# One more block of queries and keys as a unit of tokens with groups of seven products, turned on PE, and the attention heads run later

## The chip, the cores and the metric

The kernel runs on one core of a Trainium2 chip. A core has a matrix engine (PE), a vector engine (DVE), a scalar engine (ACT), a general engine (POOL) and a queue engine that issues most loads (SP). The metric is the device time of one execution in microseconds (us); less is better.

## The reference

One decoder layer for 256 tokens of 2048 features. Both head groups read one projection, and their outputs are concatenated:

```
u = RMSNorm(h)
P = u @ W_in                 # columns [z | x,B,C | dt | q | k | v]
SSD heads:  conv + SiLU on x,B,C; Mamba-2 scan; gate SiLU(z); RMSNorm
attention:  16 heads of 128, causal, three dilated patterns merged
            by their softmax denominators
h = h + RMSNorm(concat(SSD, attn) @ W_out)
h = h + RMSNorm(W_down @ relu(W_up @ RMSNorm(h))^2)
```

All values are 32-bit floats. q, k and v have 2048 columns each, so four blocks of 512 columns, each with four heads.

## The kernel before

**Products.** Each 32-bit factor is split into a high part (ACT, line 147) and a low part (DVE, line 148), and a product of two factors is three matmuls: high by high, low by high, high by low. Weights come in tiles of 256 rows by 512 columns: SP loads a tile into a "raw" buffer (line 161), ACT and DVE make "hi" and "lo" of it, of which there are five buffers each. A step over 256 rows is called a k here; w_in has eight of them. There are three forms of a product:

- *features* (`gemm_features`, lines 473 and 476): the weights stand still and the tokens stream, so the result has features on the partitions. High weights take 512 columns, which hold both parts of 256 tokens, and low weights take 256. Eight matmuls of each for a k and a column block.
- *tokens*, plain (`row_tile`, lines 328 to 330): the tokens stand still and 512 weight columns stream; 12 matmuls for a k and a column block. The text calls these 12 a tile.
- *tokens*, by seven (`seven`, lines 411 to 413): for a k and two column blocks, seven products of halves replace eight, so 21 matmuls instead of 24. DVE adds up halves of the two raw tiles first (line 252: into "e" and "r"), and sums of the activations are made once for each k (lines 368 to 371).

A *unit* makes two column blocks in the tokens form over all k, some plain and some by seven; its sums lie in four "acc" results and four "more" results, and at its end they are combined on DVE (lines 421 to 424). Results lie in PSUM, which has eight banks: six of the pool "acc" (`bank()`) and two of the pool "ps" (`psmall()`).

**Queries, keys, values.** q and k are wanted with features on the partitions. Block 0 is made as features. Block 1 is made as a unit (queries and keys are its two column blocks; k = 1, 3, 5, 6 by seven), and its 16 pieces of 128 x 128 are then turned with transposes on PE (line 921). Blocks 2 and 3 are made as features (`queries`, added up at line 497 and scaled at line 896). The values are made in two units of two blocks (V0 and V2; sums at lines 966 and 967).

**Attention.** `attention` is a generator for a lane, a pair of heads, in three steps. Step 1: scores of both heads on PE (854, 855) into two "ps" banks; DVE takes masked maxima (862), ACT the exponentials (864), DVE reciprocals and scaling (866, 868). Step 2: transposes on PE (876) into two "ps" banks, copied by ACT (880). Step 3: products with the values on PE (885, 886) into one "ps" bank, split into "ah" and "al" by ACT (147) and DVE (148). `heads` puts the two lanes of a block of four heads into the queue `waiting`. `pump(n)` runs the next step of n lanes in turn; the products call it after each k or tile, by the tuple `pumps`. Every step of PE, DVE and ACT has its place in its engine's queue before the run.

**Order before.** Features of block 0; the unit QK1 of block 1; V0, in which QK1's results are turned; Q2 and K2 as features, with heads 0 and heads 1 beside them; V2; Q3 and K3 as features, with heads 2; then the first five k of w_out in two column blocks as ten plain tiles (EARLY = 5), with heads 3; then a unit with the rest of w_out's k for these two blocks. That unit begins once the pool "ap" of the heads is closed; ACT then issues the loads of "wpost" and of x (lines 1264 to 1269). Its order is k = 5, 6, 7, 8, 9, 11, 10, 13, 12, of which 6, 8, 9, 10 and 12 are by seven.

**Places beside the pools.** While no heads run, the space of attention's outputs ("ah0" and "al0", `not_yet`) holds four further raw tiles, so there are eight; the rows of a unit and the places of DVE's additions are tiles "tk" and "cT" of the middle pool.

Of the kernel before, what the change touches and what calls it, by code (L numbers as in the profile page):

```python
# [10 lines left out]
F32 = mybir.dt.float32  # L11
# [5 lines left out]
P = 128  # L17
S = 256
# [21 lines left out]
KB = 2  # L40
# [37 lines left out]
def hymba_layer(ctx: ExitStack, tc: tile.TileContext, x, norm_mix_pre, w_in, conv_w, conv_b, dt_bias, a_log,  # L78
# [239 lines left out]
    def drain():  # L318
        while waiting:
            pump()  # L320
# [104 lines left out]

    for n in (0, 2):
        plan("v", w_v, n, range(7), V_SEVENS)
    plan("out", w_out, 0, (5, 6, 7, 8, 9, 11, 10, 13, 12), (6, 8, 9, 10, 12))
    plan("out", w_out, 2, (0, 6, 1, 9, 2, 12, 3, 4, 5, 8, 7, 10), (6, 9, 12, 4, 8, 10))
    for hf in range(2):  # L430
        for n in range(0 if hf else 2, 8, 2):
# [473 lines left out]
            sums_of_acts(k)  # L905
            yield

    def place_of_sums():

        room["sum"] = mp.tile([P, 4, S], F32, name="cT", bufs=5).rearrange("p (k f) s -> p k (f s)", k=KB)  # L910

    def eight_banks():
        more = [psmall(), bank(), psmall(), bank()]
        return [bank() for _ in range(2 * NT)], more

    def turned_heads(t, dst, r, p, later):
        for _ in range(later):
# [6 lines left out]
    def keys_by_tokens(hb, order, last, acc, more):  # L924

        room["own"] = deque(mp.tile([P, NT, NB], F32, name="tk", bufs=3)[:, t] for t in range(NT))
        if hb == 1:
            place_of_sums()
            rstq.append(mp.tile([P, NT], F32, name="rstq"))
            nc.vector.tensor_scalar(rstq[0], rstd, DH ** -0.5, None, op0=ALU.mult)  # L930
        rows, both = [], []

        def ready():
            if not more:
                more.extend(f() for f in (psmall, bank, psmall, bank))
# [12 lines left out]
        unit(w_in, (COL_Q + hb * NB, COL_K + hb * NB), order_of(order, QK_SEVENS), last, acc, more,  # L948
             lambda x: combine_new([[v[:, t] for t in range(NT)] for v in rows], x), 0, (end(0), end(1)),
             ready=ready)  # L950
        return both
# [2 lines left out]

    def two_values(vb, acc, more):

        room["own"] = deque(mp.tile([P, NT, NB], F32, name="tk", bufs=3)[:, t] for t in range(NT))
        if vb:
            place_of_sums()
        values = [mp.tile([P, NT, NB], F32, name="tk", bufs=3) for _ in range(2)]  # L960

        def end(b):
# [22 lines left out]
    ap_ = ExitStack()  # L985
    ap = ap_.enter_context(tc.tile_pool(name="ap", bufs=2, side="right", reuse_waits="tile"))
# [7 lines left out]
    qk.append(keys_by_tokens(1, (0, 2, 1, 3, 4, 5, 6), (7,), *eight))  # L994
    vs = two_values(0, *eight[::-1])
    room["raw"], room["turn"] = [], 0
    att[0] = [bigr.tile([P, NK // 2, S], F32R, name=name) for name in ("ah0", "al0")]
# [12 lines left out]

# [467 lines left out]
```

## Time and profile before

| | |
|---|---|
| median of 3 runs | 1458.33 us (1457.78 to 1458.51) |
| the profiled execution | 1458.42 us, its span 1456.6 us |
| mean granted clock of PE | 0.999 |
| PE busy | 1448.5 us, 99% of the span |
| DVE busy | 1268.3 us, 87% |
| ACT busy | 897.8 us, 62% |
| HBM read and written | 248 GB/s over the span |

Times in rows are counted from the span's start. A row of the timeline has start, length, engine, line, operation, the written and read tiles, shape, count, and in brackets the idle time of the engine before it and who ended it. The length of a matmul is longer than its distance to the next, since matmuls overlap; distances between starts give what PE needs.

### The profile page before, as it was taken

What the parts mean: (1) busy time and instruction counts of PE and PEld (TensorE: products, weight loads), DVE (VectorE), ACT (ScalarE), POOL (GpSimd) and SP (SyncE); (2) the same over time, 40 slices, a digit from 0 to 9 for tenths busy, and PEclk for the clock granted to TensorE, in tenths of its full rate; (3) what the DMA queues carried; (4) which work ended last, traced back from release to release, by engine and by line L of the source; (5) the groups of instructions that cost most, each with busy time, mean ns of one, the idle gap of its engine ahead of it and who ended that gap; (6) DMA issues with size and microseconds to landing.
All of it is one profiled execution on the core that took longest, in us unless ns stands there. A gap on an engine that the chain in (4) does not pass through costs nothing.

```text
span 1456.6 us, 20308 instructions
## 1 busy us (share of the span) xinstructions
PE 1448.5 (99%) x7117; PEld 1222.2 (84%) x7117; DVE 1268.3 (87%) x1886; ACT 897.8 (62%) x1227; POOL 146.2 (10%) x214
## 2 busy tenths in 40 slices
PE   9999999999999999999999999999999999999998
PEld 8888888888888888888888888888888888888886
DVE  6798897798987686689878999999889999999997
ACT  7465665465666556556557577666454776766663
POOL 0003100211110000001100111011111111101000
PEclk9999999999999999999999999999999999999999
DMA  8766666567875486688876798678888888798854
GB/s 270 209 205 179 184 179 197 178 175 231 237 224 174 130 235 209 191 255 270 260 226 216 205 313 242 193 227 253 241 248 279 251 245 245 210 293 263 250 176 159
DMA packets 168758, 325.10 MB, mean 223 GB/s; under 512 B 15328, under 2 KB 18256, under 8 KB 168656
## 3 DMA queue, kind: packets, MB, share of 16 engines
q1 hardware_dynamic: 144496, 272.37, 58.3%
q0 software_dynamic: 16288, 37.76, 13.2%
q10 hardware_dynamic: 7872, 13.68, 2.7%
q8 instruction: 56, 0.92, 0.2%
q14 instruction: 46, 0.38, 0.1%
HBM read 319.53 MB, written 41.98 MB: 248 GB/s over the span
## 4 chain that ended last, share of the span: by engine, by line
PE 99%; DVE 0%; ACT 0%; issue 0%; ACTq 0%
PE acc L473 15%; PE acc L328 12%; PE acc L330 12%; PE acc L329 12%; PE acc L476 8%; PE acc L413 6%; PE acc L411 6%; PE acc L412 6%; PE ps L330 3%; PE ps L329 3%; PE ps L328 3%; PE ps L413 2%; PE ps L411 2%; PE ps L412 2%; PE ps L807 1%; PE acc L1385 1%
## 5 line engine op out<-in xcount | busy, mean ns | idle before, releaser
L147 ACT ACTIVATE hi<-raw 128x1024 fp32r<-128x1024 f32 (+1 forms) x392 | 409.8, 1051 | 268.6 <-PE acc L473 92.2
L148 DVE TENSOR_TENSOR lo<-raw,hi 128x1024 fp32r<-128x1024 f32 (+1 forms) x392 | 476.9, 1221 | 92.7 <-ACT hi L147 88.7
L473 PE MATMUL acc<-ua,hi 128*128 128x512 f32 x600 | 163.5, 401 | 0.0
L473 PEld LDWEIGHTS acc<-ua,hi 128*128 128x128 f32 x600 | 105.7, 189 | 16.7
L147 ACT ACTIVATE hi<-e 128x1024 fp32r<-128x1024 f32 x64 | 68.0, 1063 | 71.4 <-DVE e L252 66.3
L328 PE MATMUL acc<-hi,ua 128*128 128x512 f32 x248 | 98.4, 397 | 0.0
L330 PE MATMUL acc<-hi,ua 128*128 128x512 f32 x248 | 96.8, 390 | 0.0
L476 PEld LDWEIGHTS acc<-ua,lo 128*128 128x128 f32 x600 | 88.2, 189 | 10.3
L329 PE MATMUL acc<-lo,ua 128*128 128x512 f32 x248 | 96.7, 390 | 0.0
L476 PE MATMUL acc<-ua,lo 128*128 128x256 f32 x600 | 90.8, 281 | 0.0
L328 PE MATMUL acc<-hi,sh 128*128 128x512 f32 x224 | 88.4, 395 | 0.0
L330 PE MATMUL acc<-hi,sl 128*128 128x512 f32 x224 | 87.3, 390 | 0.0
L329 PE MATMUL acc<-lo,sh 128*128 128x512 f32 x224 | 87.2, 389 | 0.0
L148 DVE TENSOR_TENSOR lo<-e,hi 128x1024 fp32r<-128x1024 f32 x64 | 77.9, 1218 | 0.0
L473 PE MATMUL acc<-uc,hi 128*128 128x512 f32 x240 | 68.5, 397 | 0.0
L411 PE MATMUL acc<-hi,ah 128*128 128x512 f32 x174 | 67.8, 389 | 0.0
L412 PE MATMUL acc<-lo,ah 128*128 128x512 f32 x174 | 67.7, 389 | 0.0
L413 PE MATMUL acc<-hi,al 128*128 128x512 f32 x174 | 67.7, 389 | 0.0
L148 DVE TENSOR_TENSOR lo<-ha,hi 128x1024 fp32r<-128x1024 f32 x43 | 52.4, 1220 | 6.0 <-ACT hi L147 5.7
L147 ACT ACTIVATE hi<-ha 128x1024 fp32r<-128x1024 f32 x43 | 45.3, 1057 | 18.3 <-PE acc L330 9.8
L330 PEld LDWEIGHTS acc<-hi,ua 128*128 128x128 f32 x248 | 46.6, 188 | 10.0
L328 PEld LDWEIGHTS acc<-hi,ua 128*128 128x128 f32 x248 | 46.6, 188 | 9.4 <-ACT ua L149 0.3
(543 smaller groups left out, 3510.9 us busy)
## 6 DMA issues: line engine op xcount, KB each, us to landing
raw<-in_w_in_dram SPq DMA_DIRECT2D x167, 512.0 KB, 3.9
raw<-in_w_down_dram SPq DMA_DIRECT2D x72, 512.0 KB, 5.2
raw<-in_w_up_dram SPq DMA_DIRECT2D x65, 512.0 KB, 4.6
raw<-in_w_out_dram SPq DMA_DIRECT2D x38, 512.0 KB, 5.0
pair<-in_w_up_dram POOLq DMA_DIRECT2D x56, 256.0 KB, 5.3
pair<-in_w_down_dram POOLq DMA_DIRECT2D x50, 256.0 KB, 6.3
raw<-pair SPq DMA_DIRECT2D x46, 256.0 KB, 4.6
ha<-in_w_up_dram SPq DMA_DIRECT2D x20, 512.0 KB, 5.7
```

What stands on the lines that cost most here:

```text
L147: return (nc.scalar.activation(hi, src, AF.Copy), nc.vector.tensor_tensor(lo, src, hi.bitcast(F32), op=ALU.subtract))
L148: nc.vector.tensor_tensor(lo, src, hi.bitcast(F32), op=ALU.subtract))
L328: nc.tensor.matmul(dst, a_h[:, r, ts], hi[:, j], start=begin and j == 0, stop=False)
L329: nc.tensor.matmul(dst, a_h[:, r, ts], lo[:, j], start=False, stop=False)
L330: product[t] = nc.tensor.matmul(dst, a_l[:, r, ts], hi[:, j], start=False, stop=end and j == KB - 1)
L411: nc.tensor.matmul(dst, a_h, hi[:, j], start=own and first, stop=False)
L412: nc.tensor.matmul(dst, a_h, lo[:, j], start=False, stop=False)
L413: nc.tensor.matmul(dst, a_l, hi[:, j], start=False, stop=own and last)
L473: nc.tensor.matmul(acc[f], hi[:, j, f * P:(f + 1) * P], u(k0 + j), start=k0 + j == 0, stop=False, skip_group_check=True)
L476: nc.tensor.matmul(acc[f][:, 0], lo[:, j, f * P:(f + 1) * P], u(k0 + j)[:, 0], start=False, stop=k0 + j == NK - 1, skip_group_check=True)
L807: nc.tensor.matmul(p[:, c, r], bc[:, r, c * P:(c + 1) * P], xdt[:, c, r], start=True, stop=True)
L1385: nc.tensor.transpose(p[:, f * P:(f + 1) * P], r[:, f * P:(f + 1) * P], ident)
```

## The change

- Block 2's queries and keys become a unit like block 1's (`keys_by_tokens(2, ...)`, after V0), four k of seven by seven in the order 0, 2, 1, 3, 4, 5, 6 and then 7. Its 16 pieces are turned on PE (line 923) beside the first k of Q3.
- For these units the places of DVE's additions and one further raw tile lie in a new pool `tp` of three tiles; the pool `ap` of the heads is opened only after them. The rows of the units lie in "al0", so three further raw tiles remain instead of four: seven raw buffers in all. The banks of "acc" and "more" are dealt out the other way round.
- Heads 0 run beside Q3 and heads 1 beside K3 (features), with new `pumps`. Heads 2 and 3 both run beside the ten tiles of w_out: `heads` takes several blocks, and a lane goes on with block 3 after block 2.
- w_out's first unit has its k in the order 5, 7, 6, 9, 8, 11, 10, 13, 12, with the same five by seven.

The core of the diff:

```diff
-    plan("out", w_out, 0, (5, 6, 7, 8, 9, 11, 10, 13, 12), (6, 8, 9, 10, 12))
+    plan("out", w_out, 0, (5, 7, 6, 9, 8, 11, 10, 13, 12), (6, 8, 9, 10, 12))
...
     def eight_banks():
-        more = [psmall(), bank(), psmall(), bank()]
-        return [bank() for _ in range(2 * NT)], more
+        acc = [f() for f in (bank, psmall, bank, psmall)]
+        return acc, [bank() for _ in range(2 * NT)]
...
-            rows[:] = [mp.tile([P, NT, NB], F32, name="tk", bufs=3) for _ in range(2)]
-            both[:] = [mp.tile([P, 4, S], F32, name="cT", bufs=5) for _ in range(2)]
+            rows[:] = [not_yet[1][:, t:t + NT] for t in (0, NT)]
+            both.append(mp.tile([P, 4, S], F32, name="cT", bufs=5))
+            both.append(mp.tile([P, 4, S], F32, name="cT", bufs=5) if hb == 1 else
+                        mp.tile([P, NT, NB], F32, name="tk", bufs=3).rearrange("p t (f s) -> p (t f) s", s=S))
...
-    def heads(hb, qT, kT, v):
+    def heads(*blocks):
+        def lane(j):
+            for i, (hb, qT, kT, v) in enumerate(blocks):
+                if i:
+                    yield
+                yield from attention(ap, 4 * hb + j, qT[:, j:j + 2], kT[:, j:j + 2],
+                                     v[:, :, j * DH:(j + 2) * DH].rearrange("p t (j d) -> p t j d", j=2))
         for j in (0, 2):
-            waiting.append(attention(ap, 4 * hb + j, qT[:, j:j + 2], kT[:, j:j + 2],
-                                     v[:, :, j * DH:(j + 2) * DH].rearrange("p t (j d) -> p t j d", j=2)))
+            waiting.append(lane(j))
...
-    room["raw"], room["turn"], room["acts"] = [t[:, k:k + KB] for t in not_yet for k in (0, KB)], 0, act_u
+    room["raw"], room["turn"], room["acts"] = [not_yet[0][:, k:k + KB] for k in (0, KB)] + [more_raw], 0, act_u
...
     vs = two_values(0, *eight[::-1])
+    qk.append(keys_by_tokens(2, (0, 2, 1, 3, 4, 5, 6), QK_SEVENS, (7,), *eight))
...
-    heads(0, *qk[0], vs[0])
-    q2 = queries(COL_Q + 2 * NB, rbq, (1,0,1,1,0,1,1,1))
+    for _ in range(NT):
+        bank()
+    heads((0, *qk[0], vs[0]))
+    q3 = queries(COL_Q + 3 * NB, rbq, (1, 2, 1, 0, 1, 1, 2, 1))
     drain()
-    heads(1, *qk[1], vs[1])
-    qk.append((q2, queries(COL_K + 2 * NB, rbc, (1, 1, 0))))
-    drain()
+    heads((1, *qk[1], vs[1]))
+    qk.append((q3, queries(COL_K + 3 * NB, rbc, (1, 1, 0, 1, 1, 1, 1, 0))))
...
-    heads(2, *qk[2], vs[2])
-    qk.append(keys_too(3, (1, 0)))
-    heads(3, *qk[3], vs[3])
+    for _ in range(NT):
+        bank()
+    heads(*((hb, *qk[hb], vs[hb]) for hb in (2, 3)))
...
-            row_tiles(w_out, b * NB, [k], acc[b::2], part, k == 0, False, pumps=1,
+            row_tiles(w_out, b * NB, [k], acc[b::2], part, k == 0, False, pumps=(1, 1, 1, 1, 1, 2, 1, 2, 1, 1)[2 * k + b],
                       fetch=fetch_next)
```

Three places in the queues show what moves. The first is PE after V2. Before, the features of Q3 followed, and between the scores of heads 2's lane 0 (the first four rows; "ps" are the two banks) and those of lane 2 (the last four) stood two k of features:

```order
L854 MATMUL ps<-cT 128x128
L855 MATMUL ps<-cT 128x256
L854 MATMUL ps<-cT 128x128
L855 MATMUL ps<-cT 128x256
L473 MATMUL acc<-ua,hi 128x512 x8
L476 MATMUL acc<-ua,lo 128x256 x8
L473 MATMUL acc<-ua,hi 128x512 x8
L476 MATMUL acc<-ua,lo 128x256 x8
L854 MATMUL ps<-cT 128x128
L855 MATMUL ps<-cT 128x256
L854 MATMUL ps<-cT 128x128
L855 MATMUL ps<-cT 128x256
```

Now the tiles of w_out follow ("sh" and "sl" are the two parts of the SSD output), and between these scores stands one tile. Its last three matmuls and lane 2's scores:

```order
L328 MATMUL acc<-hi,sh 128x512
L329 MATMUL acc<-lo,sh 128x512
L330 MATMUL acc<-hi,sl 128x512
L854 MATMUL ps<-tk,cT 128x128
L855 MATMUL ps<-tk,cT 128x256
L854 MATMUL ps<-tk,cT 128x128
L855 MATMUL ps<-tk,cT 128x256
```

Lane 2's scores, which use the two "ps" banks again, have moved one k closer to those of lane 0.

The second place is DVE from the end of V2 to the maxima of the first scores. Before:

```order
L966 TENSOR_TENSOR tk<-acc,tk 128x512
L148 TENSOR_TENSOR lo<-raw,hi 128x1024
L966 TENSOR_TENSOR tk<-acc,tk 128x512 x2
L148 TENSOR_TENSOR lo<-raw,hi 128x1024 x4
L862 ISA sm,mx<-ps,cst 128x128
L862 ISA mx 128x1
L862 ISA sm,mx<-ps,cst 128x256
L862 ISA mx 128x1
L862 ISA sm,mx<-ps,cst 128x128
```

Now:

```order
L963 TENSOR_TENSOR tk<-acc,tk 128x512
L148 TENSOR_TENSOR lo<-raw,hi 128x1024
L963 TENSOR_TENSOR tk<-ps,tk 128x512 x2
L148 TENSOR_TENSOR lo<-raw,hi 128x1024 x4
L862 ISA sm,mx<-ps,cst 128x128
L862 ISA mx 128x1
L862 ISA sm,mx<-ps,cst 128x256
L862 ISA mx 128x1
L862 ISA sm,mx<-ps,cst 128x128
```

The order of additions (966 is now 963), low parts and maxima stayed the same, while the low parts are now those of w_out.

The third place is where heads 0 run. On PE, their second steps (transposes, line 876, of lane 0 and then of lane 2). Before, in Q2:

```order
L876 MATMUL ps<-ident,sm 128x128 x6
L473 MATMUL acc<-ua,hi 128x512 x8
L476 MATMUL acc<-ua,lo 128x256 x8
L473 MATMUL acc<-ub,hi 128x512 x8
L476 MATMUL acc<-ub,lo 128x256 x8
L876 MATMUL ps<-ident,sm 128x128 x6
L473 MATMUL acc<-uc,hi 128x512 x8
L476 MATMUL acc<-uc,lo 128x256 x8
```

Now, in Q3:

```order
L876 MATMUL ps<-ident,sm 128x128 x6
L473 MATMUL acc<-uc,hi 128x512 x2
L476 MATMUL acc<-uc,lo 128x256 x2
L473 MATMUL acc<-uc,hi 128x512
L876 MATMUL ps<-ident,sm 128x128 x4
L473 MATMUL acc<-uc,hi 128x512
L876 MATMUL ps<-ident,sm 128x128 x2
L476 MATMUL acc<-uc,lo 128x256 x2
```

Two k of features stood between the two lanes' transposes, and now five matmuls do, and one more stands inside those of lane 2.

On DVE, the low parts ahead of the first maxima of heads 0. Before:

```order
L148 TENSOR_TENSOR lo<-raw,hi 128x1024
L966 TENSOR_TENSOR tk<-acc,tk 128x512 x2
L148 TENSOR_TENSOR lo<-raw,hi 128x1024 x4
L862 ISA sm,mx<-ps,cst 128x128
L862 ISA mx 128x1
```

Now:

```order
L148 TENSOR_TENSOR lo<-raw,hi 128x1024
L943 TENSOR_TENSOR al_3683<-ps,al_3683 128x512
L148 TENSOR_TENSOR lo<-raw,hi 128x1024 x8
L862 ISA sm,mx<-ps,cst 128x128
L862 ISA mx 128x1
```

Four low parts in a row stood there behind the last additions for the values (966), and now eight stand behind the last addition for the new unit's keys (943).

More of the change, by code (lines that the diff above doesn't have):

```diff
@@ L906, in sums_ahead, with own_places @@
             yield
-    def place_of_sums():
-        room["sum"] = mp.tile([P, 4, S], F32, name="cT", bufs=5).rearrange("p (k f) s -> p k (f s)", k=KB)
+    def own_places(tiles):
+        own, total = tiles
+        room["own"] = deque(own[:, t] for t in range(NT))
+        room["sum"] = total
     def eight_banks():
-        more = [psmall(), bank(), psmall(), bank()]
-        return [bank() for _ in range(2 * NT)], more
+        acc = [f() for f in (bank, psmall, bank, psmall)]
+        return acc, [bank() for _ in range(2 * NT)]
     def turned_heads(t, dst, r, p, later):
@@ L922, in turned_heads, with keys_by_tokens @@
         nc.scalar.activation(dst[:, :, t * P:(t + 1) * P], p.rearrange("p (f s) -> p f s", f=4), AF.Copy)
-    def keys_by_tokens(hb, order, last, acc, more):
-        room["own"] = deque(mp.tile([P, NT, NB], F32, name="tk", bufs=3)[:, t] for t in range(NT))
+    def keys_by_tokens(hb, order, sevens, last, acc, more):
         if hb == 1:
-            place_of_sums()
             rstq.append(mp.tile([P, NT], F32, name="rstq"))
@@ L946, in end @@
             return at_end
-        unit(w_in, (COL_Q + hb * NB, COL_K + hb * NB), order_of(order, QK_SEVENS), last, acc, more,
+        unit(w_in, (COL_Q + hb * NB, COL_K + hb * NB), order_of(order, sevens), last, acc, more,
              lambda x: combine_new([[v[:, t] for t in range(NT)] for v in rows], x), 0, (end(0), end(1)),
@@ L984, in hymba_layer @@
     not_yet = [bigr.tile([P, 2 * KB, NB], F32, name=name) for name in ("ah0", "al0")]
-    ap_ = ExitStack()
-    ap = ap_.enter_context(tc.tile_pool(name="ap", bufs=2, side="right", reuse_waits="tile"))
+    tp_ = ExitStack()
+    tp = tp_.enter_context(tc.tile_pool(name="tp", bufs=1, side="right", reuse_waits="tile"))
+    more_raw, *of_sums = [tp.tile([P, KB, NB], F32, name=f"tp{i}") for i in range(3)]
+    own_places(of_sums)
     room["sums"] = [v[:, k:k + KB] for k in range(0, NK // 2, KB) for v in att[1]]
-    room["raw"], room["turn"], room["acts"] = [t[:, k:k + KB] for t in not_yet for k in (0, KB)], 0, act_u
+    room["raw"], room["turn"], room["acts"] = [not_yet[0][:, k:k + KB] for k in (0, KB)] + [more_raw], 0, act_u
     waiting.append(sums_ahead())
@@ L993, in hymba_layer @@
     eight = eight_banks()
-    qk.append(keys_by_tokens(1, (0, 2, 1, 3, 4, 5, 6), (7,), *eight))
+    qk.append(keys_by_tokens(1, (0, 2, 1, 3, 4, 5, 6), QK_SEVENS, (7,), *eight))
     vs = two_values(0, *eight[::-1])
+    qk.append(keys_by_tokens(2, (0, 2, 1, 3, 4, 5, 6), QK_SEVENS, (7,), *eight))
     room["raw"], room["turn"] = [], 0
+    tp_.close()
     att[0] = [bigr.tile([P, NK // 2, S], F32R, name=name) for name in ("ah0", "al0")]
-    heads(0, *qk[0], vs[0])
-    q2 = queries(COL_Q + 2 * NB, rbq, (1,0,1,1,0,1,1,1))
+    ap_ = ExitStack()
+    ap = ap_.enter_context(tc.tile_pool(name="ap", bufs=2, side="right", reuse_waits="tile"))
+    for _ in range(NT):
+        bank()
+    heads((0, *qk[0], vs[0]))
+    q3 = queries(COL_Q + 3 * NB, rbq, (1, 2, 1, 0, 1, 1, 2, 1))
     drain()
-    heads(1, *qk[1], vs[1])
-    qk.append((q2, queries(COL_K + 2 * NB, rbc, (1, 1, 0))))
-    drain()
+    heads((1, *qk[1], vs[1]))
+    qk.append((q3, queries(COL_K + 3 * NB, rbc, (1, 1, 0, 1, 1, 1, 1, 0))))
+    own_places([mp.tile([P, 4, S], F32, name="cT", bufs=5).rearrange("p (k f) s -> p k (f s)", k=KB) for _ in range(2)])
     vs += two_values(2, *eight_banks())
-    heads(2, *qk[2], vs[2])
-    qk.append(keys_too(3, (1, 0)))
-    heads(3, *qk[3], vs[3])
+    for _ in range(NT):
+        bank()
+    heads(*((hb, *qk[hb], vs[hb]) for hb in (2, 3)))
     del room["own"], room["sum"]
```

5 lines of the change are left out of this document (removed).

## The prediction

> **What bounds the kernel now.** I read the page first, for the bound; then the chain of work that ended last; then a table of stretches, one for each stage around the change; then the timeline of single engines at the places where the new order differs. The page says:
>
> ```profile
> span 1456.6 us, 20308 instructions
> PE 1448.5 (99%) x7117; PEld 1222.2 (84%) x7117; DVE 1268.3 (87%) x1886; ACT 897.8 (62%) x1227; POOL 146.2 (10%) x214
> PE 99%; DVE 0%; ACT 0%; issue 0%; ACTq 0%
> ```
>
> PE is busy for 1448.5 of 1456.6 us and 99% of the chain runs over it. So two things alone count: how long PE's own work is, and whether a new wait opens in it. DVE, at 87%, is the engine that could open one. The stages (columns: length, then busy time of PE, PEld, DVE, ACT, POOL with counts, granted clock, DMA share, GB/s):
>
> ```profile
> 360.20:401.25 41.05, 41.05 (x184) 34.02 (x183) 40.27 (x54) 24.90 (x30) 7.03 (x10) 1.00 0.91 249
> 401.25:443.92 42.67, 42.67 (x198) 35.45 (x196) 38.61 (x45) 29.03 (x34) 4.07 (x6) 1.00 0.70 197
> 443.92:501.75 57.83, 57.83 (x346) 51.46 (x344) 36.88 (x90) 34.17 (x70) 1.35 (x2) 1.00 0.56 164
> 501.75:542.61 40.86, 40.86 (x183) 33.82 (x182) 35.65 (x42) 23.92 (x26) 4.09 (x6) 1.00 0.77 217
> 542.61:593.87 51.26, 51.26 (x302) 45.35 (x301) 34.56 (x61) 28.96 (x51) 0.00 (x0) 1.00 0.64 197
> ```
>
> In order: the unit of the second block's queries and keys (QK1); the first unit of values (V0), which also turns QK1's results on PE; the third block's queries and keys as features (Q2, K2) with two blocks of heads; the second unit of values (V2); the fourth block's queries and keys (Q3, K3) with one block of heads. PE is busy in all of each, at full clock.
>
> **The work that PE loses and gains.** The third and fifth rows are the same two features, with two blocks of heads and with one. Their difference, 57.83 - 51.26 = 6.57 us, is one block of heads on PE, and 51.26 - 6.57 = 44.69 us is a pair of features alone. That is removed for block 2. In its place comes a unit like QK1; V2 is a unit with nothing beside it, 40.86 us. Its 16 transposes are the difference between V0 and V2: 42.67 - 40.86 = 1.81 us. The heads keep their length wherever they run. Sum: -44.69 + 40.86 + 1.81 = -2.02 us. All of it is on the path, since PE has no slack.
>
> **The new unit's cover.** A group of seven costs DVE more than PE, so the unit lasts 40.86 us only if DVE starts it with a lead. Rows of DVE around the end of V0, which is where the new unit begins (443.92 is its first matmul's time; the first row is the low part of the unit's second tile, the other that of tiles three to six):
>
> ```profile
> 442.37 1.21 DVE L148 TENSOR_TENSOR lo<-raw,hi 128x1024 fp32r<-128x1024 f32 x1
> 444.73 4.79 DVE L148 TENSOR_TENSOR lo<-raw,hi 128x1024 fp32r<-128x1024 f32 x4
> ...
> 443.24 0.39 PE L328 MATMUL acc<-hi,uc 128*128 128x512 f32 x1
> 443.92 0.61 PE L473 MATMUL acc<-ua,hi 128*128 128x512 f32 x2
> ```
>
> Three matmuls of 512 columns take 0.68 us (443.24 to 443.92), 0.227 each, 2.72 for the 12 of a plain tile, 4.76 for the 21 of a seven. The second tile's low part is done at 443.58 and would be used at about 446.9: a lead of 3.3 us. Each plain tile adds 2.72 - 1.14 = 1.58 (four low parts in 4.79 us, 1.14 a step after the first); four come before the first two sevens and two before the last two. A seven in this projection takes DVE three low parts of 1.14, one of 0.6 and four or five additions of 0.6, up to 6.4, so two cost 3.3. The lead stays above 3 us: no stall. QK1, with DVE 40.27 of 41.05 busy, shows that this runs without a wait. The seven raw buffers instead of eight I cost at nothing for the same lead; without it each late load would cost its lateness.
>
> **Heads 2 and 3 beside the first products of w_out.** Here a wait is added. After V2 the order on DVE is as before: the last sums of the values, four low parts, then the first masked maximum (L862). Rows of before, where heads 2 start at the same point:
>
> ```profile
> 545.31 3.48 DVE L148 TENSOR_TENSOR lo<-raw,hi 128x1024 fp32r<-128x1024 f32 x3
> 549.60 1.23 DVE L148 TENSOR_TENSOR lo<-raw,hi 128x1024 fp32r<-128x1024 f32 x1 [0.81 <-ACT hi L147]
> 550.74 0.28 DVE L862 CUSTOM_DVE_ANT_0 sm<-ps,cst 128x128 f32<-128x128 f32 x1
> 550.95 0.42 DVE L862 CUSTOM_DVE_ANT_0 sm<-ps,cst 128x256 f32<-128x256 f32 x1
> 551.51 0.42 DVE L862 CUSTOM_DVE_ANT_0 sm<-ps,cst 128x256 f32<-128x256 f32 x1
> ...
> 545.38 0.38 PE L854 MATMUL ps<-cT 128*128 128x128 f32 x2
> 552.28 0.39 PE L854 MATMUL ps<-cT 128*128 128x128 f32 x2
> ```
>
> The scores of lane 0 stand in the two "ps" banks from 545.38; DVE has read the first bank at about 551.3. The scores of lane 2 need these banks and came at 552.28, behind two tiles, so nothing waited. Now they come behind one. The lengths, from the heads of block 3 in the same stage:
>
> ```profile
> 593.86 0.40 PE L328 MATMUL acc<-hi,sh 128*128 128x512 f32 x1
> 596.61 0.38 PE L854 MATMUL ps<-cT 128*128 128x128 f32 x2
> 597.73 0.58 PE L328 MATMUL acc<-hi,sh 128*128 128x512 f32 x1
> 598.15 0.40 PE L329 MATMUL acc<-lo,sh 128*128 128x512 f32 x1
> ```
>
> A step of scores takes 597.73 - 596.61 = 1.12, and its next matmul 0.42 instead of 0.23. Set on the old clock: 542.61 + 2.72 + 1.31 + 2.72 = 549.36 is when PE reaches lane 2's scores, and 551.3 when the bank is free: a wait of 2.0 us. Behind the waiting matmul stands all of PE's queue; DVE is ahead and only gains by it. Ends: 0, if the low parts come 2 us sooner because w_out's load is not the one that ACT waited for; 4, if the fourth of them slips by a landing. I take 2.0 since order and engines are the same, and 0.2 for later steps, where transposes follow the other lane's maximum closely: 2.2.
>
> **Heads 0 beside Q3.** Before, the two transposing steps were two k apart (457.71 and 463.96); now the second stands five matmuls behind the first, and eight low parts in a row stand ahead of the first maximum.
>
> ```profile
> 457.71 0.82 PE L876 MATMUL ps<-ident,sm 128*128 128x128 f32 x6
> 463.96 0.82 PE L876 MATMUL ps<-ident,sm 128*128 128x128 f32 x6
> 448.28 1.28 ACT L864 ACT_TABLE_LOAD   x1
> 449.76 0.40 ACT L864 ACTIVATE sm<-sm,mx 128x128 f32<-128x128 f32 x1 [0.20 <-DVE mx L862]
> 451.11 0.49 ACT L864 ACTIVATE sm<-sm,mx 128x256 f32<-128x256 f32 x1
> 459.35 0.84 ACT L880 ACTIVATE pT<-ps 128x384 f32<-128x384 f32 x2
> ```
>
> Let lane 0's scores start at 0. The last of the eight low parts waits for one of the five buffers, which frees there: ACT's high part 1.06, DVE's low part done at 2.5, maxima to 3.7. PE: scores 1.3, tile of 2.8, scores, tile, first transposes at 8.2. ACT has by then eight exponentials (0.58 and 0.68 with their read-outs) and two high parts; the last exponential ends at about 11, the first copy of transposed weights at 11.4. Lane 0's second head waits for lane 2's last maximum (9.2 against 8.5): 0.7. Lane 2's transposes need the bank that this copy frees: 11.5 against 10.5 to 10.9. Together 1.0 to 1.9; I take 1.5. Ends: 0, if ACT's high part goes ahead by half a tile, and 2.5, if one more lands between the exponentials. K3 with heads 1 keeps two tiles between these steps: nothing.
>
> **The output unit.** Its order has four plain tiles, then three sevens in a row (before: two in a row). From before (a seven's first addition, the next row after its last part, a plain tile's low part; then that tile on PE):
>
> ```profile
> 644.75 0.69 DVE L252 TENSOR_TENSOR e<-raw 128x512 f32<-128x512 f32 x1
> 650.68 0.68 DVE L368 TENSOR_TENSOR r<-ah,al 128x512 f32<-128x512 f32 x1
> 651.29 1.22 DVE L148 TENSOR_TENSOR lo<-uc,hi 128x1024 fp32r<-128x1024 f32 x1
> 652.42 0.42 DVE L369 TENSOR_TENSOR r<-r 128x256 f32<-128x256 f32 x1
> ...
> 653.30 0.39 PE L329 MATMUL acc<-lo,ah 128*128 128x512 f32 x1
> ```
>
> A seven takes DVE 5.9 (644.75 to 650.68) against 4.76 on PE; after two of them the low part was done at 652.51 and used at 653.30, 0.8 us later. Now DVE begins the sums when the last head's step ends, at E, since the place of the first sum waits for PE. From there to the low part behind the third seven stand ten operations of 1024 columns, nineteen of 512, three of 256 and six of 128 (1.14, 0.6, 0.34, 0.2): 25.0 us, so done at about E + 25.2. PE has four tiles, three sevens and one matmul: 10.9 + 14.3 + 0.3 = E + 25.5. The lead is 0.3; I take 0.2 us of stall. Ends: 0, and 3 where DVE's start or a high part comes late.
>
> With the end of the heads ACT issues the loads of x, before ahead of the last four tiles, now at the unit's start:
>
> ```profile
> 618.06 0.45 ACTq L1268 DMA_DIRECT2D ha<-in_x_dram  x1
> ha<-in_x_dram ACTq DMA_DIRECT2D x1, 1536.0 KB, 12.0
> ```
>
> They take the DMA engines for 12 us. The weights of the three sevens are asked for as buffers come free, four tiles (10.9 us) and more ahead of their use, so I cost this at nothing; if a seven's load slips past that cover, it adds to DVE's lateness below.
>
> **Sum.** -2.02 + 2.2 + 1.5 + 0.2 = +1.9 us on the profiled execution's 1458.42 us (span 1456.6 and 1.8 around it): 1460.3. The median of the runs shown is 0.09 below it, so 1460.2. I call under 0.2% (2.9 us) no change, which is about what a measurement of this kernel tells apart: 1455.4 to 1461.2.
>
> **Rivals.** *The waits do not come.* Then the gain stands alone: 1458.33 - 2.02 = 1456.3, with partial waits up to 1458.3. For it: no stage here shows PE waiting. Against: both waits follow from orders that are fixed before the run, with durations from this trace.
>
> *The output unit's third seven is late (slower).* The lead there is 0.3 us, so DVE's lateness beyond that is PE's, one for one. Seen: in this stage DVE has no gap at all between additions. The result is slower from 1.3 us of stall on (1460.2 - 0.2 + 1.3 = 1461.3); if DVE begins 2.8 us late, one tile on PE, 2.5 us are lost: 1462.5.
>
> *The clock drops during a wait.* PE's records at the end (windows: columns as above):
>
> ```profile
> 1450.40 1.13 PE L1330 MATMUL ps<-mw,dg 128*128 128x512 f32 x2 [1.70 <-ACT dg L1329]
> ...
> 1447.70:1450.40 2.70, 1.01 (x3) 0.18 (x1) 2.00 (x5) 1.42 (x4) 0.00 (x0) 1.00 0.54 190
> 1453.50:1454.00 0.50, 0.00 (x0) 0.00 (x0) 0.00 (x0) 0.00 (x0) 0.00 (x0) 0.80 1.06 373
> 1454.00:1455.00 1.00, 0.00 (x0) 0.00 (x0) 0.00 (x0) 0.00 (x0) 0.00 (x0) 0.50 0.43 162
> ```
>
> An idle stretch of 1.7 us kept 1.00; after the last matmul (to 1451.53) the clock went to 0.50 about 2.3 us later. A wait of 2.0 lies between. If the clock then stays at half for as long as the wait again and a little more, say 3 us, 1.5 us are lost: 1461.7. [...]
>
> [...]
>
> **Chances.** The forecast 0.56; waits absent or mostly so 0.17; output unit late 0.2; clock 0.07. The forecast's own range is 1458.5 to 1462, of which a quarter is above 1461.2. Of the second case a third is put under 1455.4, for which PE's work must be another 0.9 us shorter than counted. Of the third, 0.16 lies above 1461.2. So faster 0.05, same 0.58, slower 0.14 + 0.16 + 0.07 = 0.37. The range takes the second case from 1456.0 and the third up to 1464.0, which leaves about 0.15 outside.
>
> **What would show it.** Right: the unit of block 2 takes 40.9 us with no PE wait; an idle row of about 2 us on PE before lane 2's scores, released by L862, in the stage of w_out; one of 0.7 to 1.9 in sum on the transposes in Q3, released by L862 or the copy L880; DVE without gaps in the output unit. Wrong: a unit longer than 41.5 (DVE or loads late), no wait at the scores (low parts earlier), more than 1.1 us of PE waiting at the third seven, or a granted clock under 1.00 anywhere between 360 and 700 us.

## The result and the profile after

The changed kernel takes 1462.28 us in the median of seven runs (1459.8 to 1464.39), the kernel before beside it 1458.33 us (1457.68 to 1458.53). The ratio is 1.0028, its interval 1.0018 to 1.0038: slower by 0.28%. That is above the 0.2% taken as measurable, so the change made the kernel slower. (The ratios in this text are worked out from the single executions and need not be those of the medians.) The profiled execution takes 1462.42 us, 4.00 more than the one before, and the waiting is in one place. The page after:

```profile
span 1460.6 us, 20239 instructions
PE 1449.4 (99%) x7057; PEld 1219.1 (83%) x7057; DVE 1283.0 (88%) x1906; ACT 905.9 (62%) x1236; POOL 146.5 (10%) x214
PE 96%; DVE 3%; ACT 1%; issue 0%; ACTq 0%
```

PE has 60 instructions less than before and yet is busy for 0.9 us more, which says that some of its work ran slower. In the chain of work that ended last, DVE and ACT now hold 4%. The stages (columns as in the prediction): QK1 and V0 together; the new unit; Q3 and K3 with two blocks of heads; V2; the ten tiles of w_out with two blocks of heads; the start of the output unit.

```profile
360.37:444.38 84.01, 83.94 (x378) 69.04 (x377) 80.52 (x103) 53.62 (x63) 10.16 (x14) 1.00 0.86 243
444.38:485.18 40.80, 40.80 (x181) 33.80 (x180) 39.99 (x49) 26.06 (x30) 0.00 (x0) 1.00 0.57 165
485.18:545.09 59.91, 59.91 (x362) 53.16 (x361) 36.80 (x88) 35.80 (x73) 1.36 (x2) 1.00 0.56 161
545.09:585.90 40.81, 40.81 (x183) 33.78 (x182) 36.78 (x45) 22.79 (x25) 4.10 (x6) 1.00 0.76 212
585.90:631.64 45.74, 42.74 (x209) 35.44 (x208) 28.85 (x75) 28.64 (x60) 2.71 (x4) 0.96 0.66 206
631.64:660.00 28.36, 28.36 (x128) 23.48 (x127) 28.04 (x44) 17.30 (x22) 2.73 (x4) 1.00 0.84 252
```

The fifth row shows PE idle for 3.00 of 45.74 us (the first for 0.07, which is taken up with QK1 below, the others for none), and only there is the granted clock below 1.00. PE's timeline in that stage:

```profile
592.24 0.39 PE L329 MATMUL acc<-lo,sh 128*128 128x512 f32 x1
592.47 0.39 PE L330 MATMUL acc<-hi,sl 128*128 128x512 f32 x1
595.85 0.49 PE L854 MATMUL ps<-tk,cT 128*128 128x128 f32 x2 [3.00 <-DVE mx L862]
596.18 0.60 PE L855 MATMUL ps<-tk,cT 128*128 128x256 f32 x2
...
598.03 0.63 PE L329 MATMUL acc<-lo,sh 128*128 128x512 f32 x1
598.46 0.63 PE L330 MATMUL acc<-hi,sl 128*128 128x512 f32 x1
```

The scores of heads 2's lane 2 wait 3.00 us for lane 0's maximum (L862). By starts, 3.385 us (592.47 to 595.85) instead of 0.227 costs 3.16 us. Behind it a matmul step takes 0.43 (598.03 to 598.46) instead of 0.23. The windows around that stretch:

```profile
596.75:597.00 0.25, 0.25 (x4) 0.25 (x3) 0.25 (x2) 0.25 (x1) 0.00 (x0) 0.83 1.18 344
597.00:597.25 0.25, 0.25 (x3) 0.17 (x2) 0.25 (x2) 0.25 (x1) 0.00 (x0) 0.50 0.99 320
...
600.25:600.50 0.25, 0.25 (x3) 0.20 (x2) 0.25 (x2) 0.25 (x1) 0.00 (x0) 0.84 0.92 147
```

A window of 0.25 us with a mean of 0.83 was at full clock for two thirds of it, so the clock fell to half at 596.92; the same reading of the last row puts its return at 600.33. That is 3.41 us at half, 1.7 us of PE's time. Against the prediction's terms, stage by stage, in us:

| stage | PE's work by its terms | waits forecast | measured |
|---|---|---|---|
| start to the end of V0 | 443.92 | 0 | 444.38 |
| new unit | 40.86 | 0 | 40.80 |
| Q3, K3, two blocks of heads, 16 transposes | 44.69 + 13.14 + 1.81 = 59.64 | 1.5 | 59.91 |
| V2 | 40.86 | 0 | 40.81 |
| ten tiles, two blocks of heads | 27.2 + 13.14 = 40.34 | 2.2 | 45.74 |
| output unit's wait | 0 | 0.2 | 0 |

Measured less work is 0.46 - 0.06 + 0.27 - 0.05 + 5.40 = 6.02, and with the 2.02 us that PE's work became shorter +4.00, which is the difference between the two executions. Of the 5.40, 3.16 is the wait and 1.7 the clock. The other 0.5 was not taken apart, but it belongs to the stage and not to this execution: with the waits taken off, two traces of later runs have 0.7 (the changed kernel again) and 0.9 (the sums of QK1 where they were) above 40.34 there.

**What made the wait 3 us.** ACT and DVE ahead of the maximum:

```profile
587.30 1.06 ACT L147 ACTIVATE hi<-raw 128x1024 fp32r<-128x1024 f32 x1 [2.01 <-DMA raw<-in_w_out_dram]
588.58 1.06 ACT L147 ACTIVATE hi<-raw 128x1024 fp32r<-128x1024 f32 x1 [0.22 <-DMA raw<-in_w_out_dram]
589.54 1.32 ACT L964 ACTIVATE tk<-tk,rstd 128x512 f32<-128x512 f32 x2
590.77 1.04 ACT L147 ACTIVATE hi<-raw 128x1024 fp32r<-128x1024 f32 x1
591.72 1.32 ACT L964 ACTIVATE tk<-tk,rstd 128x512 f32<-128x512 f32 x2
592.95 1.04 ACT L147 ACTIVATE hi<-raw 128x1024 fp32r<-128x1024 f32 x1
594.02 1.23 DVE L148 TENSOR_TENSOR lo<-raw,hi 128x1024 fp32r<-128x1024 f32 x1 [0.94 <-ACT hi L147]
595.16 0.28 DVE L862 CUSTOM_DVE_ANT_0 sm<-ps,cst 128x128 f32<-128x128 f32 x1
```

ACT stands until 587.30 for a tile of w_out. From there it works to 593.99, with one pause of 0.22 us, on four high parts and the scaling of the values (L964); DVE's last low part and the maximum follow. So a late load moves everything down to PE's scores. In the kernel before ACT stood for a load at this place too:

```profile
544.16 1.06 ACT L147 ACTIVATE hi<-raw 128x1024 fp32r<-128x1024 f32 x1 [2.81 <-DMA raw<-in_w_in_dram]
```

That is 1.55 us behind the end of V2 (542.61), against 1.40 here (587.30 and 585.90). But from there to the maximum it had three high parts to make, and here four: one tile more landed late. One high part more is 1.1 us, about the difference between the wait of 2.0 that was forecast and the 3.0.

### The profile page after: what moved, and what is told of

It reads as the page before. It is cut to its first block, busy times and chain, and to the rows that moved or that the text cites. A ratio compares the mean times of both kernels' runs of the same rounds, so it can differ in the third digit from the quotient of the medians.

```text
span 1460.6 us, 20239 instructions
## 1 busy us (share of the span) xinstructions
PE 1449.4 (99%) x7057; PEld 1219.1 (83%) x7057; DVE 1283.0 (88%) x1906; ACT 905.9 (62%) x1236; POOL 146.5 (10%) x214
## 4 chain that ended last, share of the span: by engine, by line
PE 96%; DVE 3%; ACT 1%; issue 0%; ACTq 0%
PE acc L473 13%; PE acc L328 12%; PE acc L330 12%; PE acc L329 12%; PE acc L476 7%; PE acc L412 6%; PE acc L411 6%; PE acc L413 6%; PE ps L328 3%; PE ps L330 3%; PE ps L329 3%; PE ps L411 2%; PE ps L412 2%; PE ps L413 2%; DVE lo L148 1%; PE ps L807 1%
## 5 line engine op out<-in xcount | busy, mean ns | idle before, releaser
L147 ACT ACTIVATE hi<-raw 128x1024 fp32r<-128x1024 f32 (+1 forms) x388 | 405.1, 1050 | 256.5 <-PE acc L330 85.6
L148 DVE TENSOR_TENSOR lo<-raw,hi 128x1024 fp32r<-128x1024 f32 (+1 forms) x388 | 471.9, 1220 | 83.8 <-ACT hi L147 80.6
L473 PE MATMUL acc<-ua,hi 128*128 128x512 f32 x520 | 141.6, 401 | 0.0
L473 PEld LDWEIGHTS acc<-ua,hi 128*128 128x128 f32 x520 | 91.5, 189 | 14.4
L476 PEld LDWEIGHTS acc<-ua,lo 128*128 128x128 f32 x520 | 76.5, 189 | 8.9
L476 PE MATMUL acc<-ua,lo 128*128 128x256 f32 x520 | 78.7, 281 | 0.0
L473 PE MATMUL acc<-uc,hi 128*128 128x512 f32 x208 | 59.8, 399 | 0.0
```

What stands on the lines that cost most here:

```text
L147: return (nc.scalar.activation(hi, src, AF.Copy), nc.vector.tensor_tensor(lo, src, hi.bitcast(F32), op=ALU.subtract))
L148: nc.vector.tensor_tensor(lo, src, hi.bitcast(F32), op=ALU.subtract))
L473: nc.tensor.matmul(acc[f], hi[:, j, f * P:(f + 1) * P], u(k0 + j), start=k0 + j == 0, stop=False, skip_group_check=True)
L476: nc.tensor.matmul(acc[f][:, 0], lo[:, j, f * P:(f + 1) * P], u(k0 + j)[:, 0], start=False, stop=k0 + j == NK - 1, skip_group_check=True)
```

## The experiments

In each diff the lines changed are those of the kernel named. The kernel before ran beside each group, on the same chip: 1458.5 us for the first four, 1458.56 for the next three, 1458.62 for the last three.

**One tile more between the two lanes' scores.** The changed kernel with

```diff
-pumps=(1, 1, 1, 1, 1, 2, 1, 2, 1, 1)[2 * k + b],
+pumps=(1, 0, 1, 1, 2, 2, 1, 2, 1, 1)[2 * k + b],
```

> The changed kernel with one edit: beside w_out's first tiles the scores of heads 2's lane 2 come after the third tile, two tiles behind those of lane 0, instead of after the second. Theory W (the wait on the 'ps' banks, and the halved clock that it brings, are what the change lost): PE reaches these scores 2.7 us later, so the wait of 3.0 us shrinks to about 0.4, the granted clock stays at 1.00 there, and 3.16 - 0.4 + 1.7 = 4.4 us come back: 1462.3 - 4.4 = 1457.9, a little under the kernel before, and the runs spread less. Rival U (the new unit, or loads that the change moved, cost the time, and the wait only stands where PE would have lost it anyway): the time stays at 1462 within 1 us, and the wait opens again later.

It took 1460.2 us (1458.96 to 1462.08), a ratio of 1.0013 with an interval of 1.0004 to 1.0021; theory W said 1457.9. The clock did not fall: the mean granted in the traced execution is 0.999, and behind the two waits matmuls of 512 columns start 0.23 us apart (597.83 to 598.06 and 603.11 to 603.34). Its waits of PE (us in total, times, longest):

```profile
PE ps L876 <- DVE mx L862: 1.6, 1, 1.6
PE ps L854 <- DVE mx L862: 1.0, 1, 1.0
```

The wait at the scores fell from 3.0 to 1.0 and the clock's loss went with it. The forecast of 0.4 was 0.6 too low, and the load that ACT stands for came 0.7 later in this trace (2.10 us behind the end of V2 instead of 1.40). And a second wait of 1.6 opened, as the rival had it: lane 0's transposes now come one tile behind lane 2's scores and need a bank that lane 2's maximum must first have read, and DVE makes a low part (1.22 us) between that lane's two heads. So with one tile between the lanes' steps the two banks "ps" had no slack in either place.

**The same spacing in the kernel before, where w_in's products follow.** Once with one k of features between the two lanes' scores, about as in the changed kernel (a tile), once with 12 matmuls, less than one k, which is as close as they could be put.

```diff
-    qk.append(keys_too(3, (1, 0)))
+    qk.append(keys_too(3, (1, 1, 0, 0, 1, 0, 1, 0)))
```

```diff
-    qk.append(keys_too(3, (1, 0)))
+    qk.append(keys_too(3, (2, 0, 0, 0, 1, 0, 1, 0)))
```

> The kernel before with one edit: beside Q3 the scores of heads 2's lane 2 come one k behind those of lane 0 instead of two. This is the changed kernel's wait without the rest of the change. Theory W: PE reaches the scores at 546.50 + 0.19 + 2.79 = 549.5 on the old clock and the bank is free at 551.3, so a wait of 1.8 us opens; if a wait under 2 us leaves the clock alone, 1458.3 + 1.8 = 1460.1; if it halves the clock, 1461.8. Rival U: no wait, 1458.3.

> As before, with the scores of lane 2 put as close behind lane 0's as the program's planner lets them be, 12 matmuls. Theory W: PE reaches them at 549.0 on the old clock, a wait of 2.3 us. If the clock falls only after about 3 us of idle time, 1460.7; if after 2.3, another 1.7 us are lost, 1462.3. Rival U: no wait, 1458.3.

With one k: 1460.09 us (1459.43 to 1462.61), a ratio of 1.0012, interval 1.0003 to 1.0021; with 12 matmuls 1460.47 us (1459.47 to 1463.74), 1.0015, interval 1.0006 to 1.0025. The wait on PE in the first:

```profile
PE ps L854 <- DVE mx L862: 1.5, 1, 1.5
```

and 1.3 us in the second, both with a mean granted clock of 0.999 in the execution that was traced. The first is near its forecast of 1.8, so spacing alone, with no other part of the change, brings the wait. The second is 1.0 shorter than forecast. In its trace the load that ACT stands for came 0.48 us behind the end of V2 (542.77 and 542.29), 1.07 sooner than the 1.55 of the kernel before, on which the forecast was reckoned; so here too the landing accounts for the difference. In the changed kernel the same spacing costs 1.9 to 3.0, and there it is w_out's loads that ACT waits for.

**The old order of the output unit.** The changed kernel with

```diff
-    plan("out", w_out, 0, (5, 7, 6, 9, 8, 11, 10, 13, 12), (6, 8, 9, 10, 12))
+    plan("out", w_out, 0, (5, 6, 7, 8, 9, 11, 10, 13, 12), (6, 8, 9, 10, 12))
```

> The changed kernel with w_out's first unit in the order of before (k = 5, 6, 7, 8, 9, ...): one plain k, a seven, a plain k, two sevens. If DVE can begin the sums only when the last step of the heads ends, as the prediction counts, the first seven's sums are done 8.4 us after that end and wanted after 7.1: a wait of 1.3, and 0.3 behind the two sevens, together 1.6 us slower than the changed kernel, 1463.9. If DVE begins earlier, no wait: 1462.3, and the new order is worth nothing.

It took 1464.51 us (1464.2 to 1465.67), a ratio of 1.0043 with an interval of 1.0028 to 1.0058. The expectation had 1463.9, with waits of 1.3 and 0.3 at the sevens. Its waits of PE:

```profile
PE ps L854 <- DVE mx L862: 2.9, 1, 2.9
PE acc L412 <- DVE lo L148: 1.2, 1, 1.2
PE acc L411 <- ACT hi L147: 0.4, 1, 0.4
```

DVE's first sum in that unit, from the timeline of the same run:

```profile
631.44 0.69 DVE L252 TENSOR_TENSOR e<-raw 128x512 f32<-128x512 f32 x1 [2.15 <-PE ps L886]
```

DVE stands 2.15 us until PE has done the last product of the heads (L886) and only then begins the sums. That is the prediction's start E. With a group of seven as second item of the order PE then waits for DVE, with the new order it doesn't.

**The changed kernel again, unaltered.**

> The changed kernel itself, to be compared on one chip with the two kernels below. Both theories: 1462.3 within 1 us. If the halved clock follows the wait each time, the row of PE's wait of about 3 us is followed by some 3.3 us at a granted clock of 0.50; if it is an accident of one run, the clock stays at 1.00 and the time is 1460.6.

It took 1461.78 us (1459.62 to 1464.81, ten runs), a ratio of 1.0022 with an interval of 1.0013 to 1.0031. The profiled execution took 1459.62 us, and in it the wait is shorter. PE's and ACT's timelines:

```profile
592.37 0.39 PE L330 MATMUL acc<-hi,sl 128*128 128x512 f32 x1
594.68 0.49 PE L854 MATMUL ps<-tk,cT 128*128 128x128 f32 x2 [1.93 <-DVE mx L862]
...
589.58 1.06 ACT L147 ACTIVATE hi<-raw 128x1024 fp32r<-128x1024 f32 x1 [0.56 <-DMA raw<-in_w_out_dram]
590.55 1.32 ACT L964 ACTIVATE tk<-tk,rstd 128x512 f32<-128x512 f32 x2
591.77 1.04 ACT L147 ACTIVATE hi<-raw 128x1024 fp32r<-128x1024 f32 x1
```

The stretches around it:

```profile
590.00:595.00 5.00, 3.07 (x14) 2.21 (x14) 3.38 (x9) 3.50 (x7) 0.00 (x0) 1.00 1.01 363
595.00:600.00 5.00, 5.00 (x29) 4.26 (x28) 4.57 (x23) 4.56 (x16) 0.00 (x0) 1.00 0.67 239
```

ACT's last high part starts at 591.77 here and at 592.95 above, 1.18 earlier; the wait is 1.07 shorter, and the clock holds. So in these two traces the wait that the change adds is 1.9 and 3.0 us, as the loads land, and the clock's 1.7 us come only with the longer. The other nine runs have no trace, but seven of the ten show a mean granted clock of 0.996 to 0.998 and took 1461.22 to 1464.81 us, and the three at 0.999 took 1459.62 to 1460.54. What the two above 1464 us lost besides is not known.

**Heads later and farther apart.** The changed kernel with

```diff
-pumps=(1, 1, 1, 1, 1, 2, 1, 2, 1, 1)[2 * k + b],
+pumps=(0, 1, 0, 1, 1, 2, 2, 1, 2, 2)[2 * k + b],
```

> The changed kernel with heads 2's first scores behind w_out's second tile and lane 2's behind the fourth; the later steps follow a tile after each other, the last two both behind the tenth tile. Theory W (two lanes meet on two banks whenever less time lies between them than DVE needs): both waits go, that of the scores (3.0 us, 1.0 with the lanes apart alone) and that of lane 0's transposes (1.6 with the lanes apart alone), the clock stays at 1.00, and what remains of the change is the shorter work, -2.0, against 0.5 lost in QK1 and V0 and up to 0.5 at the output unit, where one more split stands ahead of DVE's sums: 1457.5. Rival (DVE is short of time in this stage, so a wait that is removed opens again further on): 1460.

It took 1458.88 us (1457.62 to 1460.48), a ratio of 0.9998 with an interval of 0.999 to 1.0007. One wait is left in the stages around the change:

```profile
PE ps L876 <- DVE mx L862: 0.3, 1, 0.3
```

So the waits beside w_out's tiles, with the clock's loss that follows from them, are the loss against the kernel before, to within this interval. But the 2.02 us that PE's work became shorter do not all appear: 1457.5 was expected, 1.4 less than measured. One part of that is in QK1, and the next run takes it out; another is the stage of w_out's tiles, which with its wait taken off is 1.0 longer here than its terms.

**The sums of QK1 where they were.** The kernel of the last run, with the places of QK1's additions taken from the tile "tk", as before, and those of the new pool only from V0 on.

```diff
-    own_places(of_sums)
+    own_places((mp.tile([P, NT, NB], F32, name="tk", bufs=3), of_sums[1]))
...
-    vs = two_values(0, *eight[::-1])
+    own_places(of_sums); vs = two_values(0, *eight[::-1])
```

> The same with one more edit: in QK1 the sums of activations and the sevens' last parts use a tile of the middle pool again, as in the kernel before, and the new pool's tile only from V0 on. Theory P (the new place is free only at 350 us, so the first two sums of activations start there instead of at 307 and one of them, 1.9 us of DVE, falls into QK1, where DVE comes late to a seven): the gap of 0.34 us on PE at 392 goes and the time falls by 0.4 to 1457.1. Rival (the seven raw buffers instead of eight make the loads late in QK1): the gap stays.

It took 1457.81 us (1456.94 to 1460.33), a ratio of 0.9998 with an interval of 0.9989 to 1.0007. That is the best of all medians here, 0.75 us below the kernel before beside it, but not told apart from it, nor from the last run: the two intervals are nearly the same. What the edit did is read from the trace. The sums of activations, by source line (count; shortest, median and longest in ns; first and last start), in the changed kernel:

```profile
L368 DVE TENSOR_TENSOR tp<-ua x2: 685/688/692, 350.3 to 352.4; 128x512 f32<-128x512 f32 x2
L368 DVE TENSOR_TENSOR tp<-uc x1: 686/686/686, 363.7 to 363.7; 128x512 f32<-128x512 f32 x1
```

and in this run:

```profile
L368 DVE TENSOR_TENSOR tk<-ua x2: 687/690/692, 307.1 to 308.9; 128x512 f32<-128x512 f32 x2
L368 DVE TENSOR_TENSOR tk<-uc x1: 693/693/693, 356.7 to 356.7; 128x512 f32<-128x512 f32 x1
```

The stretch of QK1 in the changed kernel:

```profile
360.00:402.00 42.00, 41.93 (x186) 34.36 (x185) 41.69 (x59) 25.57 (x31) 6.28 (x9) 1.00 0.86 233
```

and in this run:

```profile
360.00:402.00 42.00, 42.00 (x186) 34.75 (x186) 41.23 (x55) 25.14 (x29) 6.60 (x10) 1.00 0.88 248
```

The new pool's place comes free only at about 350 us, so in the changed kernel the first sums wait 43 us and the last falls into QK1, whose DVE has no time for it: PE there is busy for 41.93 of 42 us, and here for all of them. By starts of matmuls the gap was 0.34 us, and it is gone.

**Longer waits made on purpose.** In the kernel before with one k between the lanes, DVE makes 2, 4 or 7 copies ahead of the first maximum of heads 2. The copies compute nothing that is kept. The diff for four:

```diff
+            [nc.vector.tensor_copy(sm, s[:, :3 * P]) for _ in range(4 * (h == 8 and j == 0))]
             for t, (cs, mk) in enumerate(spans):
```

> The kernel before with the scores of heads 2's two lanes one k apart, as in the earlier run that had an idle stretch of 1.5 us and 1460.1 us, and two copies of 128x384 on DVE ahead of lane 0's first maximum. They compute nothing that is kept; each is priced at 0.47 us, the 128x256 pass of L862 (0.34 a step) and half as much again less its start. So PE's wait is 1.5 + 0.9 = 2.4 us, between the 1.9 that kept the clock and the 2.9 that did not. Theory C (the clock halves when PE has stood for some length between 1.9 and 2.9 us, for about 3.3 us, which costs 1.65): 1461.0 where the limit is above 2.4, 1462.7 where it is below, and the same in all executions. [...] Rival L (the lower clock belongs to the stage of w_out, not to a wait): 1461.0 with the clock at 1.00.

> The same with four copies: a wait of 1.5 + 1.9 = 3.4 us. Theory C: the clock is halved for about 3.3 us behind the wait in every execution, 1460.1 + 1.9 + 1.65 = 1463.6. [...] Rival L: 1462.0 and the clock at 1.00.

> The same with seven copies: a wait of 1.5 + 3.3 = 4.8 us. It tells whether the time at half clock grows with the wait. Theory C with a fixed time of 3.3 us at half: 1460.1 + 3.3 + 1.65 = 1465.0; with a time at half as long as the wait and a little more (5.2 us, 2.6 lost): 1466.0. [...] Rival L: 1463.4.

They took 1460.46 us (ratio 1.0017, interval 1.0008 to 1.0027), 1460.12 (1.0013, 1.0004 to 1.0023) and 1461.2 (1.0015, 1.0005 to 1.0024). All three forecasts of the wait failed: lane 2's scores, whose place in PE's queue is planned, moved back behind more matmuls as DVE's work grew, and the waits are 1.6, 2.1 and 2.0 us. They bear on the clock all the same, by the execution that was traced of each. With four copies, PE's timeline and then the stretches where the clock changes:

```profile
554.79 0.49 PE L854 MATMUL ps<-cT 128*128 128x128 f32 x2 [2.12 <-DVE mx L862]
```

```profile
555.50:555.75 0.25, 0.25 (x2) 0.20 (x2) 0.25 (x1) 0.25 (x2) 0.00 (x0) 0.52 0.82 213
558.75:559.00 0.25, 0.25 (x3) 0.19 (x2) 0.00 (x0) 0.00 (x0) 0.00 (x0) 0.65 0.90 344
```

With seven, the same two views:

```profile
558.08 0.49 PE L854 MATMUL ps<-cT 128*128 128x128 f32 x2 [1.96 <-DVE mx L862]
```

```profile
558.00:560.00 2.00, 1.92 (x10) 1.65 (x11) 2.00 (x9) 1.20 (x6) 0.00 (x0) 1.00 0.91 263
560.00:562.00 2.00, 2.00 (x16) 1.91 (x15) 1.35 (x10) 1.52 (x4) 0.00 (x0) 1.00 0.82 213
```

Behind a wait of 2.12 us the clock was at half from 555.51 to 558.93, 3.42 us; behind one of 1.96 it stayed at 1.00. With four copies the traced execution (1462.3) and one other (1462.6) stand apart from the eight that took 1459.41 to 1460.7; so the slower time did not come in all executions, as theory C has it. The rival that ties the lower clock to the stage of w_out falls, since here it is beside Q3. What the waits' lengths say of the clock is taken up in the last section.

## Why the prediction was right or wrong

The range (1456 to 1464) held the time, but by luck: 1462.3 lies above the forecast's own range, which ends at 1462, in the part that was added for a late output unit, and that unit was not late. The likeliest case, no change at 1460.2, did not come: the time is 2.1 us higher and slower by more than 0.2%.

- *The unit, its lead, V2 (-2.02 us of work).* Right: 40.80 us against 40.86 with no wait, 40.81 for V2. The loads, with seven raw buffers, cost nothing there. (A seven on DVE, put at up to 6.4 us, is 7.0 by the same terms where it has five additions; the lead stays above 3 us even so.)
- *The wait at lane 2's scores (2.0, ends 0 and 4).* Right in place, releaser and mechanism; the size was 1.9 in one execution and 3.0 (3.16 by starts) in the other. The step that failed is "I take 2.0 since order and engines are the same": the upper end's cause, a low part that slips by a landing, is what happened, and it cost 1.1 and not 2. The later steps, put at 0.2, did not wait. Why w_out's tiles land late stays open; one that ACT waited for took 7.56 us from its issue (579.64) to its landing (587.20).
- *The clock (chance 0.07, 1.5 us).* Wrong in its chance, near in its price: 1.7 us. The chance was the author's estimate, and so were the 3 us at half, which no row of before shows; the trace has 3.41. The step that failed read the two idle stretches, 1.7 and 2.3, as a length beyond which the clock falls, and set a wait of 2.0 between them; nothing was asked about the wait's own upper end, at which the same rows speak for a fall. What the traces show of its fall is taken up below.
- *Heads 0 beside Q3 (1.5, ends 0 and 2.5).* Missed: PE has no wait in the stage, which took 0.27 us more than its work. The failed step was that the last low part "waits for one of the five buffers, which frees there", that is, when lane 0's scores start:

```profile
500.15 1.06 ACT L147 ACTIVATE hi<-raw 128x1024 fp32r<-128x1024 f32 x1 [1.15 <-PE acc L473]
502.38 0.28 DVE L862 CUSTOM_DVE_ANT_0 sm<-ps,cst 128x128 f32<-128x128 f32 x1
```

  The buffer that this high part needs is that of the high weights, and PE reads it last at L473, about 0.75 us before lane 0's scores (500.90), while the low products still run. So the first maximum comes 1.48 us after the scores and not 2.5, and the later collisions of the lanes do not arise. That was the lower end given.
- *Places of the additions (nothing).* Wrong by up to 0.46 us: the prediction costs the seven raw buffers by the new unit's lead and has no term for the places in the new pool; it did not ask when that space becomes free for QK1. Of the 0.46, 0.29 lies in QK1 and V0, where the gap of 0.34 by starts was shown to come from these places (the rest there is 0.05 shorter); 0.17 lies ahead of QK1 and is within the spread of runs.
- *Output unit (0.2).* Right: no wait, DVE busy for 28.04 of 28.36 us in the last row of the stages. The same unit in the old order waits 1.6 us by its waits, which bears out the start at E.
- *The rivals.* "The waits do not come" fell with the 3 us row; nearly that kernel was then run with the waits moved away, and at 1457.81 it stands 1.5 above the 1456.3 worked out for it. PE's work did become shorter, and the two banks took back more than that. But the shorter work is not what larger matmuls bring. 16 plain tiles of 2.72 us are 43.5, only 1.2 less than the 44.69 of the features, and the turning takes 1.81 of that back. It is the four sevens, 0.68 us less each than the two tiles that they replace, that bring 2.7 us, and only with these is the change a gain for PE.

So two errors of opposite sign (1.2 us too much in Q3, 1.2 too little at the scores) cancel, which is luck. What is left of the 2.1 us is the clock's 1.7, the 0.46 up to the end of V0 and 0.5 in the stage of w_out's tiles, less the 0.4 for later steps and the output unit that were not needed. The 0.5 goes against "The heads keep their length wherever they run": with two blocks beside the ten tiles it does not quite hold, for a reason that stays open.

## What to carry to other kernels

A wait that replaces busy time on PE has to be priced with the clock: in the traces here 3.41 or 3.42 us at half clock, 1.7 us of PE's time, came behind waits of 2.12, 2.91 and 3.00 us, and none behind those of up to 1.96. When places are moved to another pool, look at when that space becomes free for each user, the earliest too. Two lanes that share two PSUM banks need time for DVE's full pass between their steps: with one tile (2.72 us) between the scores of the two, PE waited 1.9 to 3.0 us, a tile more left 1.0 and moved the collision to the next step (1.6), and with all of the steps spread 0.3 was left.

## What was not expected of the hardware

The clock's fall follows neither the wait's length alone nor a fixed delay. PE's longest wait in the stages around the heads and the granted clock behind it, from the trace of each run:

| run | PE's wait, us | clock behind it |
|---|---|---|
| changed kernel | 3.00 (592.85 to 595.85) | half from 596.92 to 600.33, 3.41 us |
| old output order | 2.91 (592.43 to 595.34) | half from 596.10 to 599.52, 3.42 us |
| four copies | 2.12 (552.67 to 554.79) | half from 555.51 to 558.93, 3.42 us |
| seven copies | 1.96 (556.12 to 558.08) | 1.00 up to 564 |
| changed kernel again | 1.93 (592.75 to 594.68) | 1.00 up to 605 |
| two copies | 1.6 | 1.00 up to 566 |

In mid-program the length alone would fit: waits of 2.12 us and more are followed by half the clock, those of up to 1.96 are not. But it does not fit at the end of the run "Heads later and farther apart". There the longest idle stretch is 1.70 us, the last matmul ends at 1453.58, and the clock falls 0.7 us later, at 1454.30:

```profile
1452.46 1.12 PE L1340 MATMUL ps<-mw,dg 128*128 128x512 f32 x2 [1.70 <-ACT dg L1339]
1454.00:1454.50 0.50, 0.00 (x0) 0.00 (x0) 0.22 (x1) 0.22 (x1) 0.00 (x0) 0.80 0.63 225
```

The delay differs too. In mid-program the clock fell 4.1 us after PE stopped in the changed kernel, 3.7 in the run with the old output order and 2.8 in the one with four copies, each time when PE was at work again (1.07, 0.76 and 0.72 us after the wait's end). After the last matmul it fell 0.7 us later in the run above, 3.4 later with seven copies (1454.42 to 1457.78) and 1.6 later in the changed kernel (1455.52 to 1457.08), whose fall the row

```profile
1457.00:1457.50 0.50, 0.00 (x0) 0.00 (x0) 0.00 (x0) 0.00 (x0) 0.00 (x0) 0.58 1.03 377
```

shows. What sets the moment of the fall, and so whether a wait of 2 to 3 us costs the clock in every execution, no run here shows: the two waits near 3 us that were traced, of 2.91 and 3.00, both lost it.
